# Ten gate and value pairs per layer from seven half-block products

## The chip, the cores and the metric

One core of one Trainium2 chip runs the kernel; the other cores are idle. The metric is the device time of the whole program in microseconds. The kernel before took 1496.4 us (median of 3 runs, 1495.83 to 1497.2). The engines are named as in the profile: PE (TensorE, matmuls) with PEld (its weight loads), DVE (VectorE), ACT (ScalarE), POOL (GpSimd) and SP (SyncE, which issues the DMAs).

## The reference

A trunk of four residual steps over 512 positions of width 1024, in two layers. Layer 0 mixes with a gated short convolution and differential attention, layer 1 with stick-breaking attention; each layer then attends into 256 memory tokens and applies a gated feed-forward block. Only the feed-forward block is touched here:

```python
D_FF = 2816                       # w_up: 1024 x 5632, w_down: 2816 x 1024

def rmsnorm(x, g):
    y = x * lax.rsqrt(jnp.mean(x * x, axis=-1, keepdims=True) + EPS)
    return y * g

def causal_dwconv(x, w):          # width 3, over positions
    ...

def conv_ffn(h, w_up, w_conv, w_down):
    u = causal_dwconv(h @ w_up, w_conv)
    gate, val = jnp.split(u, 2, axis=-1)
    return (jax.nn.silu(gate) * val) @ w_down

x = x + conv_ffn(rmsnorm(x, norm_ffn[l]), ffn_w_up[l], ffn_conv[l], ffn_w_down[l])
```

All is fp32.

## The kernel before

Activations lie transposed: 8 tiles `x` of 128 channels by 512 positions. Every fp32 operand is carried as two float32r parts, `hi` (a rounded copy, made by ACT) and `lo` (operand minus `hi`, made by DVE; `split`). A product of two operands is then three matmuls into one PSUM accumulator: `hi`x`hi`, `hi`x`lo`, `lo`x`hi`.

Weights come from HBM in slots of 128 x 1024, in the order in which they are used (`weight_groups`), through three `raw` buffers (`loads`); `prep` splits each slot into a `hi` and a `lo` tile (five buffers each). `lin` walks a group: for each chunk of 128 output columns it takes an accumulator `acc` (three PSUM buffers), and `lin_stream` issues 24 matmuls (8 blocks of 128 input channels, three each) of 128 x 128 weights against 512 positions. PSUM has three more pools: `sc` (two buffers), `tr` (two) and `pv` (one), which the attention stages use and the feed-forward stage leaves alone.

In the feed-forward stage of a layer (`ffn`) the up-projection has 22 pairs, chunk j (gate) and chunk 22 + j (value). The kernel before loads two pairs as one group `U` (a = 0 to 10). The normalising factor of a position, 1/rms, is a row (`rrow`) that is known late; the operand split into `hs` tiles is therefore x times the gain alone, and each finished chunk is multiplied by `rrow` on DVE (`c<-acc,rrow`). Three convolution steps follow (one on ACT, two on DVE), Silu on ACT for a gate, the product of the two on DVE, and a split for the down-projection. The down-projection runs in three blocks of 8, 8 and 6 of the 22 inner tiles, `D`; each adds its result to `x` (`x<-x,acc`). The first down block follows up group 4 (pairs 0 to 9), the others come near the end.

The order of work on each engine is fixed when the program is built: `Issue.run` plays streams of operations (loads, prep, one stream per accumulator, follow-up work) against costs and latencies, and appends to each engine's list the operation that can start first, with a priority where several can. On the chip every engine then takes its list strictly in that order and waits on semaphores. So a change in one place may reorder what comes later.

Names in the profile are those of tiles, with the buffer numbers left out. Lines that matter: L441 `tensor_tensor`, L449 `scalar_tensor_tensor`, L426 a copy or cast on ACT, L429 an ACT function, L479 the matmul, L483 a transpose. In the changed kernel these lines stand three lower (L444, L452, L429, L432, L482, L486).

Of the kernel before, what the change touches and what calls it, by code (L numbers as in the profile page):

```python
# [32 lines left out]
SORDER = ("q0", "v0", "q1", "q2", "v1", "q3")  # L33


def weight_groups():

    def c(*starts):
# [20 lines left out]
    def common(l):  # L59
        for a in range(2):  # L60
            g.append((f"Q{a}_{l}", "x_w_q", l, ks, c(*range(4 * a, 4 * a + 4))))
        for a in range(2):
            g.append((f"XO{a}_{l}", "x_w_out", l, ks[4 * a:4 * a + 4], c(*range(8))))

        def up(a):
            g.append((f"U{a}_{l}", "ffn_w_up", l, ks, c(2 * a, 22 + 2 * a, 2 * a + 1, 22 + 2 * a + 1)))

        def dn(a, b):
            kk = list(range(8 * a, min(8 * a + 8, 22)))
            g.append((f"D{a}{b}_{l}", "ffn_w_down", l, kk, c(*range(4 * b, 4 * b + 4))))  # L70

        for a in range(5):
            up(a)
        dn(0, 0)
        dn(0, 1)
        for a in range(5, 9):
            up(a)
        dn(1, 0)
        up(9)
        dn(1, 1)  # L80
        up(10)
        dn(2, 0)
        dn(2, 1)

    kv(0)
    common(0)
# [14 lines left out]


GROUPS = weight_groups()
GN = {g[0]: i for i, g in enumerate(GROUPS)}
NSLOT = [len(g[3]) * len(g[4]) * P // SLOT for g in GROUPS]
FIRST = [sum(NSLOT[:i]) for i in range(len(GROUPS) + 1)]

# [36 lines left out]
POW_WAIT = 0.0  # L144

PREP_FIRST, SUM_FIRST, SUM = 0.45, 3.2, 1.5
PE_RATE, PE_FIX = 2400.0, 0.0133


# [228 lines left out]
def trunk(ctx: ExitStack, tc: tile.TileContext, xT: bass.AP, memT: bass.AP, wts: bass.AP, par: bass.AP, outT: bass.AP):  # L378
# [251 lines left out]
    def loads():  # L630
        for gi in range(len(GROUPS)):
            for d in extra.get(gi, ()):
                yield from d()
            for s in range(NSLOT[gi]):
# [10 lines left out]
                    yield dma(raw.v(), src, SLOT)  # L645
                raws[gi, s] = raw

    def prep(groups):
        for gi in groups:
            for s in range(NSLOT[gi]):  # L650
                hi, lo = yield [AL(pHI, F32R, (P, SLOT), parts=2), AL(pLO, F32R, (P, SLOT), parts=2)]
                if gi == 0:
                    for j in range(2):
                        js = slice(j * 512, j * 512 + 512)
                        yield Until(lambda: (gi, s, j) in raws)
                        raw = raws[gi, s, j]
                        yield act(hi[:, js].p(j), raw[:, js].p(j))
                        yield tt(lo[:, js].p(j), raw[:, js].p(j), hi[:, js].p(j).f32(), ALU.subtract)
                        prepped[gi, s, j] = (hi, lo)
                else:  # L660
                    yield Until(lambda: (gi, s) in raws)
                    raw = raws[gi, s]
                    yield act(hi, raw)
                    yield tt(lo, raw, hi.v().f32(), ALU.subtract)
                    prepped[gi, s, 0] = prepped[gi, s, 1] = (hi, lo)
                free(raw)

    def lin_stream(gi, m, kind, A, ps, done, n):
# [29 lines left out]
        if sub is not None:  # L698
            spawn(sub, 1.0)
        fin[gi] = fin.get(gi, 0) + 1  # L700


    used_k = {}
# [588 lines left out]
    def ffn(l, xin, xout, last):  # L1292
        N = norm_x(xin, f"norm_ffn{l}", True)
        acts, own, gate_t = {}, {}, {}

        def up_done(a):
            def done(m, ps):
                j = 2 * a + m // 2
                gate = m % 2 == 0
                u = yield AL(pC)  # L1300
                yield Until(lambda: "rrow" in N)
                yield tt(u, ps, N["rrow"], ALU.mult)
                free(ps)
                t = yield AL(pG)
                yield from conv3(u, f"ffn_conv{l}", j if gate else 22 + j, 44, t)
                free(u)
# [18 lines left out]
                    acts[j] = o  # L1325
            return done

        def up(a):
            yield from lin(f"U{a}_{l}", "f", N["A"], up_done(a))

        names = [xin, ("f0", l), ("f1", l), xout]

        def dn(a, b):
            base = add_x(names[a], names[a + 1], 4 * b)

            def done(m, ps):
                k = 4 * b + m
                if last and a == 2 and k == KD - 1:

                    yield Until(lambda: (names[a], k) in F)  # L1340
                    x = F[names[a], k]
                    for js in (slice(0, S // 2), slice(S // 2, S)):
                        yield tt(x[:, js], x[:, js], ps[:, js], ALU.add)
                        yield dma(outT[k][:, js], x[:, js], S // 2)
                    free(ps)
                    return
                yield from base(m, ps)
# [3 lines left out]
            if b == 1:  # L1351
                def fr():
                    yield lin_done(f"D{a}0_{l}", f"D{a}1_{l}")
# [4 lines left out]
        for a in range(5):  # L1358
            yield from up(a)
        yield from dn(0, 0)  # L1360
        yield from dn(0, 1)
        for a in range(5, 9):
            yield from up(a)
        yield from dn(1, 0)
        yield from up(9)
        yield from dn(1, 1)
        yield from up(10)

        def nfree():
            yield lin_done(f"U10_{l}")  # L1370
            hs_free(N)
            yield Until(lambda: 21 in acts)
            free(N["r"], N["rrow"])
        spawn(nfree(), 0.1)
        yield from dn(2, 0)
        yield from dn(2, 1)


    so, sown, sqk, sv, sv_own = {}, {}, {}, {}, {}
# [272 lines left out]
```

## Time and profile before

| | |
|---|---|
| median of 3 runs | 1496.4 us |
| the profiled execution | 1496.61 us |
| its span, first to last instruction | 1494.8 us |
| PE busy | 1488.9 us, 6968 matmuls |
| DVE busy | 1022.3 us, 1625 instructions |
| ACT busy | 725.2 us, 1193 instructions |
| granted clock of PE | 1.00 |

The profile is of one execution. A line of a timeline has the start and length in us, the engine, the source line, the operation, output<-inputs, the shape and a count. A line of the list of groups has the count, then the busy time and the mean length of one in ns. Matmuls are pipelined, so their recorded lengths overlap; what one costs in a row of them is the distance of their starts.

### The profile page before, as it was taken

The page shows a single profiled execution, that of the slowest core. Times are in us where ns is not written, and L with a number is a line of the kernel's source. Part 1 is how long each engine was busy: PE and PEld are TensorE (multiplying, and loading weights), DVE is VectorE, ACT ScalarE, POOL GpSimd, SP SyncE. Part 2 cuts the span into 40 slices and gives each one's busy share as a digit, 9 for nine tenths or more (in the row PEclk, how much of TensorE's full clock was granted, in tenths as well). Part 3 has the DMA queues.
Part 4 walks back from the last instruction along what each step waited for, and adds up shares of the span by engine and source line. Part 5 has one row for each costly group of instructions (what it writes and reads, how often), then busy time and mean ns, then how long its engine had stood idle before and what let it go on. Part 6 is the DMA issues. An engine that isn't in the chain of part 4 may idle for free.

```text
span 1494.8 us, 18401 instructions
## 1 busy us (share of the span) xinstructions
PE 1488.9 (100%) x6968; PEld 1240.3 (83%) x6968; DVE 1022.3 (68%) x1625; ACT 725.2 (49%) x1193; POOL 66.1 (4%) x139
## 2 busy tenths in 40 slices
PE   9999999999999999999999999999999999999998
PEld 8888888888888888888888888888888888888887
DVE  7689767565776367555678989857657775567543
ACT  6576456443544144334477877755435443334321
POOL 3210000000000000000100000000000000000000
PEclk9999999999999999999999999999999999999999
DMA  7122436211332333233221221552212333233322
GB/s 234 57 85 71 149 119 190 92 57 57 113 107 78 98 113 90 79 113 112 86 69 59 65 92 57 145 165 85 81 61 70 100 113 113 72 98 113 95 75 85
DMA packets 42711, 146.20 MB, mean 98 GB/s; under 512 B 4864, under 2 KB 5376, under 8 KB 42624
## 3 DMA queue, kind: packets, MB, share of 16 engines
q1 hardware_dynamic: 42624, 145.04, 31.3%
q8 instruction: 55, 0.90, 0.3%
q14 instruction: 32, 0.26, 0.1%
HBM read 142.92 MB, written 2.10 MB: 97 GB/s over the span
## 4 chain that ended last, share of the span: by engine, by line
PE 94%; DVE 3%; ACT 1%; DMA 1%; issue 1%; SPq 0%; DVEq 0%
PE acc L479 85%; PE sc L479 4%; PE pv L479 3%; PE tr L483 3%; DMA raw<-wts 1%; DVE lo L441 0%; DVE g L1408 0%; ACT h L426 0%; DVE g L441 0%; DVE h L441 0%; DVE pt L441 0%; DVE c L441 0%; ACT hi L426 0%; DVE kl L449 0%; SPq L488 0%
## 5 line engine op out<-in xcount | busy, mean ns | idle before, releaser
L479 PE MATMUL acc<-hs,hi 128*128 128x512 f32 x2208 | 690.7, 391 | 0.0
L479 PEld LDWEIGHTS acc<-hs,hi 128*128 128x128 f32 x2208 | 413.4, 188 | 83.2
L479 PE MATMUL acc<-hs,lo 128*128 128x512 f32 x1104 | 430.5, 391 | 0.0
L426 ACT CAST hi<-raw 128x1024 fp32r<-128x1024 f32 (+1 forms) x264 | 273.2, 1039 | 226.2 <-PE acc L479 159.6
L441 DVE TENSOR_TENSOR lo<-raw,hi 128x1024 fp32r<-128x1024 f32 (+1 forms) x264 | 316.9, 1204 | 67.4 <-ACT hi L426 64.5
L479 PEld LDWEIGHTS acc<-hs,lo 128*128 128x128 f32 x1104 | 207.4, 188 | 41.1
L479 PE MATMUL acc<-h,hi 128*128 128x512 f32 x704 | 216.0, 389 | 0.0
L479 PE MATMUL acc<-hi,hs 128*128 128x512 f32 x544 | 176.6, 395 | 0.0
L441 DVE TENSOR_TENSOR x<-x,acc 128x512 f32<-128x512 f32 (+1 forms) x105 | 71.3, 680 | 145.0 <-PE acc L479 145.0
L479 PEld LDWEIGHTS acc<-h,hi 128*128 128x128 f32 x704 | 132.1, 188 | 27.4
L449 DVE SCALAR_TENSOR_TENSOR g<-c,pp,g 128x510 f32<-128x510 f32 (+1 forms) x176 | 131.1, 749 | 29.3 <-ACT g L429 27.1
L479 PE MATMUL acc<-h,lo 128*128 128x512 f32 x352 | 136.1, 389 | 0.0
L441 DVE TENSOR_TENSOR c<-acc,rrow 128x512 f32<-128x512 f32 x92 | 63.4, 691 | 96.6 <-PE acc L479 89.4
L429 ACT ACTIVATE g<-c,pp 128x512 f32<-128x512 f32 x88 | 63.5, 723 | 131.5 <-DVE c L441 131.5
L479 PEld LDWEIGHTS acc<-hi,hs 128*128 128x128 f32 x544 | 101.5, 188 | 20.0 <-DVE hs L449 0.3
L479 PE MATMUL acc<-lo,hs 128*128 128x512 f32 x272 | 106.5, 392 | 0.0
L479 PE MATMUL acc<-y,hi 128*128 128x512 f32 x256 | 81.0, 393 | 0.0
L479 PEld LDWEIGHTS acc<-h,lo 128*128 128x128 f32 x352 | 66.1, 188 | 13.7
L441 DVE TENSOR_TENSOR g<-g,g 128x512 f32<-128x512 f32 (+2 forms) x112 | 63.0, 571 | 3.5 <-ACT g L429 1.4
L429 ACT ACTIVATE g<-sc,rq 128x128 f32<-128x128 f32 (+7 forms) x128 | 62.2, 542 | 3.6 <-PE sc L479 3.3
L479 PEld LDWEIGHTS acc<-lo,hs 128*128 128x128 f32 x272 | 51.3, 189 | 9.8
L426 ACT CAST pt<-tr 128x128 fp32r<-128x128 f32 (+2 forms) x96 | 43.1, 457 | 30.9 <-PE tr L483 30.4
(181 smaller groups left out, 1502.5 us busy)
## 6 DMA issues: line engine op xcount, KB each, us to landing
raw<-wts SPq DMA_DIRECT2D x256, 512.0 KB, 4.1
x<-xT SPq DMA_DIRECT2D x16, 256.0 KB, 5.3
raw<-wts SPq DMA_DIRECT2D x8, 256.0 KB, 5.4
raw<-memT SPq DMA_DIRECT2D x4, 512.0 KB, 3.9
outT<-x SPq DMA_DIRECT2D x7, 256.0 KB, 2.0
outT<-x SPq DMA_DIRECT2D x2, 128.0 KB, 1.7
pp<-par SPq DMA_DIRECT2D x1, 175.5 KB, 4.7
sq<-par SPq DMA_DIRECT2D x1, 128.0 KB, 5.0
```

The lines of the kernel that those rows point to most:

```text
L426: return nc.scalar.copy(out=out.ap, in_=in_.ap)
L429: return nc.scalar.activation(out=out.ap, in_=in_.ap, func=func, scale=_raw(scale), **kw)
L441: lambda: _ve(eng).tensor_tensor(out=out.ap, in0=in0.ap, in1=in1.ap, op=op))
L449: lambda: nc.vector.scalar_tensor_tensor(out=out.ap, in0=in0.ap, scalar=_raw(scalar), in1=in1.ap, op0=op0, op1=op1))
L479: lambda: nc.tensor.matmul(out.ap, lhsT.ap, rhs.ap, start=start, stop=stop))
L483: return Op("PE", 0.109, [in_, ident_v], [out], lambda: nc.tensor.transpose(out.ap, in_.ap, ident_v.ap))
```

## The change

For ten of the 22 pairs of each layer (`SEVEN`: 8, 10, 12, 14 and 16 to 21) the two chunks are no longer formed by 48 matmuls of 512 positions. The pair is seen as a 2 x 2 block product. The positions are halved (256 each), the 8 blocks of input channels are put into two classes (even and odd), and the two chunks are the two output halves. Four such blocks of the weights times four of the activations take eight half products, and the scheme of Winograd and Strassen takes seven, with sums and differences of blocks ahead of them and additions behind. A half product is 4 blocks x 3 parts = 12 matmuls of 256 positions.

- *Weights* (`prep_halved`): both raw slots of the pair are waited for. Slot 0 is split as it is ("a"), and the last quarter alone ("d", into the two `sq` tiles); four additions or subtractions of 512 columns on DVE then turn the raw tiles into sums, which are split too ("b", "c"). Three splits of 1024 and one of 512, in place of two of 1024.
- *Activations* (`fold`): since the sums mix positions, the operand must carry `rrow`. After the last of the first eight pairs the `hs` tiles are made again, with `rrow` in them, and for each of four pairs of blocks the two halved sums are made and split. They go to tiles that the attention stages use (`kl`, `pt`, `so`, `rrow`).
- *Products* (`lin_halved`): the seven use the accumulators acc, sc, pv, tr, sc, tr, sc in this order. One copy on ACT and seven additions of 256 columns on DVE put the two chunks together in `c` tiles.
- The other pairs behind the fold (9, 11, 13, 15) lose their multiplication by `rrow`; their convolution reads the accumulator itself.
- *Order* (`FFN_ORDER`): groups of one pair in place of two; the first down block follows pair 7 instead of pair 9, and the first and second down blocks are cut into four parts of two chunks; the second stands between pairs 17 to 21.

```diff
+UP_SCALED = 8
+FFN_ORDER = ([("u", j) for j in range(8)] + [("d", 0, b) for b in range(4)] + [("u", j) for j in range(8, 17)]
+             + [("d", 1, 0), ("u", 17), ("d", 1, 1), ("u", 18), ("d", 1, 2), ("u", 19), ("u", 20), ("d", 1, 3), ("u", 21),
+                ("d", 2, 0), ("d", 2, 1)])
+SEVEN = {l: (8, 10, 12, 14, 16, 17, 18, 19, 20, 21) for l in range(2)}
...
+    def prep_halved(gi):
+        lo_, hi_ = slice(0, 512), slice(512, 1024)
+        yield Until(lambda: (gi, 1) in raws)
+        r0, r1 = raws[gi, 0], raws[gi, 1]
+        pair = [AL(pHI, F32R, (P, SLOT), parts=2), AL(pLO, F32R, (P, SLOT), parts=2)]
+        ha, la = yield pair
+        yield act(ha, r0)
+        yield tt(la, r0, ha.v().f32(), ALU.subtract)
+        prepped[gi, "a"] = (ha, la)
+        a11, a12, a21, a22 = r0[:, lo_].p(0), r0[:, hi_].p(1), r1[:, lo_].p(0), r1[:, hi_].p(1)
+        hd, ld = yield [AL(pSQ, F32R), AL(pSQ, F32R)]
+        yield act(hd, a22)
+        yield tt(ld, a22, hd.v().f32(), ALU.subtract)
+        prepped[gi, "d"] = (hd, ld)
+        yield tt(a11, a11, a21, ALU.subtract)
+        yield tt(a21, a21, a22, ALU.add)
+        yield tt(a22, a22, a11, ALU.subtract)
+        yield tt(a12, a12, a22, ALU.subtract)
+        for n, r in (("b", r1), ("c", r0)):
+            h, lo = yield pair
+            yield act(h, r)
+            yield tt(lo, r, h.v().f32(), ALU.subtract)
+            prepped[gi, n] = (h, lo)
+            free(r)
...
+    def lin_halved(gi, N, acc, done):
...
+        def product(ps, slot, off, rhs, last=True):
+            for q in range(4):
+                yield Until(lambda: (gi, slot) in prepped and N.get("folded", 0) > q)
...
+                yield mm(ps, hi[:, cs].p(j), bh, q == 0, False)
+                yield mm(ps, hi[:, cs].p(j), bl, False, False)
+                yield mm(ps, lo[:, cs].p(j), bh, False, q == 3)
...
+        yield from product(acc[:, :256], "a", 0, part(0, t1), last=False)
+        u1, u2 = yield [AL(pC, parts=2), AL(pC, parts=2)]
+        c11, c12, c21, c22 = u1[:, t1].p(0), u1[:, t2].p(1), u2[:, t1].p(0), u2[:, t2].p(1)
+        then(act(c11, acc[:, :256]), lambda: free(acc), flag("p1"))
+        p2 = yield AL(aSC)
+        yield from product(p2[:, :256], "a", 512, part(1, t1))
+        p4 = yield AL(aPV)
+        yield from product(p4[:, :256], "d", 0, sums(1, t1))
+        p6 = yield AL(aTR)
+        yield from product(p6[:, :256], "b", 512, sums(1, t2), last=False)
+        then(Until(lambda: "p1" in st), add(c12, c11, p6), lambda: free(p6), flag("p6"),
+             add(c11, c11, p2), lambda: free(p2))
+        p5 = yield AL(aSC)
+        yield from product(p5[:, :256], "b", 0, sums(0, t1))
+        p7 = yield AL(aTR)
+        yield from product(p7[:, :256], "c", 0, sums(0, t2), last=False)
+        then(Until(lambda: "p6" in st), add(c21, c12, p7), lambda: free(p7), flag("p7"),
+             add(c12, c12, p5), flag("p5"), add(c22, c21, p5), lambda: free(p5),
+             add(c21, c21, p4), lambda: free(p4), lambda: done(1, u2))
+        p3 = yield AL(aSC)
+        yield from product(p3[:, :256], "c", 512, part(1, t2))
+        then(Until(lambda: "p5" in st), add(c12, c12, p3), lambda: free(p3), lambda: done(0, u1))
...
+        def fold():
+            yield lin_done(*(f"U{j}_{l}" for j in range(UP_SCALED)))
...
+            for q in range(4):
+                b1, b2 = yield [AL(pC, parts=2), AL(pC, parts=2)]
+                for k, b in ((2 * q, b1), (2 * q + 1, b2)):
+                    yield stt(b, F[xin, k], pc(f"norm_ffn{l}", k), N["rrow"], ALU.mult, ALU.mult)
+                    N["read"] = k + 1
+                for k, b in ((2 * q, b1), (2 * q + 1, b2)):
+                    hi, lo = N["A"][k]
+                    yield from split(hi, lo, b)
+                x, y, z, w = b1[:, t1].p(0), b1[:, t2].p(1), b2[:, t1].p(0), b2[:, t2].p(1)
+                yield tt(x, y, x, ALU.subtract)
+                yield tt(y, w, y, ALU.subtract)
+                yield tt(w, w, x, ALU.subtract)
+                yield tt(z, z, w, ALU.subtract)
+                for b, (hi, lo) in zip((b1, b2), N["T"][q]):
+                    yield from split(hi, lo, b)
+                free(b1, b2)
+                N["folded"] = q + 1
```

What the change moves on the engines is seen at three places. In the rows, a tile's name carries its own number, so equal numbers are one tile.

PE, up-projection of layer 0, before: the last matmuls of one chunk and the first of the next (`hs` is the activation, `hi` and `lo` the weights).

```order
L479 MATMUL acc_4668<-hs_3653,hi_4721 128x512
L479 MATMUL acc_4668<-hs_3654,hi_4721 128x512
L479 MATMUL acc_4668<-hs_3653,lo_4722 128x512
L479 MATMUL acc_4694<-hs_3559,hi_4605 128x512
L479 MATMUL acc_4694<-hs_3560,hi_4605 128x512
L479 MATMUL acc_4694<-hs_3559,lo_4606 128x512
```

And now, in pair 8: the end of the second product and the start of the third (weights "d" in `sq`, activation sums in `kl`).

```order
L482 MATMUL sc_4672<-hs_3653,hi_4492 128x256
L482 MATMUL sc_4672<-hs_3654,hi_4492 128x256
L482 MATMUL sc_4672<-hs_3653,lo_4493 128x256
L482 MATMUL pv_4689<-kl_4311,sq_4518 128x256 x2
L482 MATMUL pv_4689<-kl_4311,sq_4519 128x256
```

Where an accumulator was filled by 24 matmuls of 512 columns, a half-wide one is filled by 12 of 256, and the next product goes to another pool.

DVE, first down block of layer 0, before: splits of weights (`lo`) and additions to the residual (`x`).

```order
L441 TENSOR_TENSOR x_1819<-x_1819,acc_4388 128x512
L441 TENSOR_TENSOR y_4503<-g_4471,y_4502 128x512
L441 TENSOR_TENSOR x_1821<-x_1821,acc_4423 128x512
L441 TENSOR_TENSOR x_1823<-x_1823,acc_4472 128x512
L441 TENSOR_TENSOR lo_4572<-raw_4461,hi_4571 128x1024
```

And now at that place: the fold for two blocks stands between them (`c` the scaled block, `hs` its new split, `kl` the split of the sums).

```order
L444 TENSOR_TENSOR c_4318<-c_4318 128x256
L444 TENSOR_TENSOR c_4318<-c_4319,c_4318 128x256
L444 TENSOR_TENSOR h_4365<-g_4329,h_4365 128x512
L444 TENSOR_TENSOR c_4319<-c_4319,c_4318 128x256
L444 TENSOR_TENSOR c_4319<-c_4319 128x256
L444 TENSOR_TENSOR lo_4378<-raw_4247,hi_4377 128x1024
L444 TENSOR_TENSOR x_1819<-x_1819,acc_4239 128x512
L444 TENSOR_TENSOR kl_4310<-c_4318,kl_4310 128x512
L444 TENSOR_TENSOR x_1821<-x_1821,acc_4276 128x512
L444 TENSOR_TENSOR kl_4311<-c_4319,kl_4311 128x512
```

The fold's rows share the list with the splits and the additions to x of the down block.

DVE, late in the up-projection of layer 0, before: splits, scalings by `rrow`, convolution steps (`g`).

```order
L441 TENSOR_TENSOR lo_5021<-raw_4896,hi_5020 128x1024
L441 TENSOR_TENSOR c_5040<-acc_4934,rrow_3756 128x512
L441 TENSOR_TENSOR lo_5036<-raw_4925,hi_5035 128x1024
L449 SCALAR_TENSOR_TENSOR g_5047<-c_5040,pp,g_5047 128x511
L449 SCALAR_TENSOR_TENSOR g_5047<-c_5040,pp,g_5047 128x510
L441 TENSOR_TENSOR g_5047<-g_5047,g_4998 128x512
```

And now: the additions of pair 19 (`c` from `tr`, `sc`, `pv`) between the weight sums (`raw`) and splits of pair 20.

```order
L444 TENSOR_TENSOR c_6129<-c_6129,tr_6159 128x256
L444 TENSOR_TENSOR raw_6051<-raw_6051 128x512
L444 TENSOR_TENSOR c_6129<-c_6129,sc_6131 128x256
L444 TENSOR_TENSOR raw_6051<-raw_6051,raw_5937 128x512
L444 TENSOR_TENSOR raw_5937<-raw_5937,raw_6051 128x512
L444 TENSOR_TENSOR c_6130<-c_6129,tr_6191 128x256
L444 TENSOR_TENSOR c_6129<-c_6129,sc_6176 128x256
L444 TENSOR_TENSOR c_6130<-c_6130,sc_6176 128x256
L444 TENSOR_TENSOR lo_6212<-raw_6051,hi_6211 128x1024
L444 TENSOR_TENSOR c_6130<-c_6130,pv_6146 128x256
```

The scalings are gone; the additions that release `tr`, `sc` and `pv` now stand in one list with another pair's weight sums and splits.

More of the change, by code (lines that the diff above doesn't have):

```diff
@@ L1356, in dn @@
                 spawn(fr(), 0.1)
[L1358 to L1367, printed above, removed]
         def nfree():
-            yield lin_done(f"U10_{l}")
+            yield lin_done(*(f"U{j}_{l}" for j in range(22)))
             hs_free(N)
+            free(*N["own"])
             yield Until(lambda: 21 in acts)
@@ L1374, in ffn @@
         spawn(nfree(), 0.1)
-        yield from dn(2, 0)
-        yield from dn(2, 1)
+        spawn(fold(), FOLD)
+        for step in FFN_ORDER:
+            yield from (up if step[0] == "u" else dn)(*step[1:])
     so, sown, sqk, sv, sv_own = {}, {}, {}, {}, {}
```

98 lines of the change are left out of this document (70 added, 28 removed).

## The prediction

> **What bounds the kernel now.** I read the page first: the engines' busy shares and the chain that ended last.
>
> ```profile
> span 1494.8 us, 18401 instructions
> PE 1488.9 (100%) x6968; PEld 1240.3 (83%) x6968; DVE 1022.3 (68%) x1625; ACT 725.2 (49%) x1193; POOL 66.1 (4%) x139
> ...
> PE 94%; DVE 3%; ACT 1%; DMA 1%; issue 1%; SPq 0%; DVEq 0%
> ```
>
> TensorE has work in all of the span, and the chain runs through it. A full busy bar alone doesn't prove a bound, because matmul records overlap; so next I read the chain in order of time, in the feed-forward stage of layer 0.
>
> ```profile
> 389.37 351.18 PE acc L479 x1549
> ```
>
> One unbroken piece: 1549 matmuls of 512 columns in 351.18 us, that is 0.2267 us each, with nothing else on the chain. Here the time is the number of matmuls times their pitch, and a shorter list of matmuls shortens the span one for one, as long as the other engines keep up. What they have left shows in the stretches of the two feed-forward stages (columns: stretch and its length; busy time of PE, PEld, DVE, ACT, POOL with counts; clock; DMA share; GB/s). The middle row is another stage, used below.
>
> ```profile
> 385.00:760.00 375.00, 375.00 (x1670) 310.67 (x1669) 237.11 (x302) 150.30 (x198) 5.55 (x14) 1.00 0.31 95
> 810.00:870.00 60.00, 59.67 (x316) 49.81 (x315) 59.19 (x102) 52.88 (x108) 5.22 (x28) 1.00 0.22 66
> 1120.00:1491.00 371.00, 371.00 (x1641) 306.81 (x1639) 227.38 (x286) 133.50 (x166) 1.01 (x1) 1.00 0.30 93
> ```
>
> The granted clock is 1.00. VectorE is busy 237 of 375 us and 227 of 371 us, so about 140 us per layer lie open on it; ScalarE and the DMA queues have more.
>
> **TensorE's part of the sum.** A gate and value pair took 2 chunks x 8 blocks x 3 matmuls = 48 of 512 columns: 48 x 0.2267 = 10.88 us. It becomes 7 products x 4 blocks x 3 = 84 of 256 columns. The columns fall by 7/8, but matmuls rise by 36, so all hangs on the pitch of a 256-wide matmul with a new weight load each. The cross-attention scores have that shape (timeline of PE: start, length, count), with the group of their weight loads behind:
>
> ```profile
> 274.00 2.04 PE L479 MATMUL sc<-y,h 128*128 128x256 f32 x15
> 275.88 0.40 PE L479 MATMUL acc<-hs,hi 128*128 128x512 f32 x1
> ...
> 1064.15 1.95 PE L479 MATMUL sc<-y,h 128*128 128x256 f32 x15
> 1065.94 0.40 PE L479 MATMUL acc<-hs,hi 128*128 128x512 f32 x1
> ...
> L479 PEld LDWEIGHTS sc<-y,h 128*128 128x128 f32 x192 | 26.0, 190 | 1.4
> ```
>
> From the first start to the next group's start: 1.79 us / 15 = 0.119 in the later run, 1.88 / 15 = 0.125 in the earlier one. I take 0.120, near the run without a hole. A pair then costs 84 x 0.120 = 10.08 us, 0.80 less, and 20 pairs (ten in each of two layers) give **-16.0 us**. The ends: at 0.119, 10.00 and -17.6; at 0.125, 10.50 and -7.6. Exactly half of a 512-wide one (0.1134) would give 9.53 and -27; no run shows it, so I keep it as a far bound. All other matmuls stay: the order has 720 more in sum, which is 20 x 36.
>
> The Trainium skill, "TensorE: Matmul & The Clock Gate", section "Back-to-back issue gap", gives 131 ns per matmul at 512 columns and 81 ns at 128 in a stream of loads and matmuls; by a straight line between them, an estimate of 98 ns at 256, a pair would go from 6.3 to 8.2 us and the change would lose some 39 us. The chain's 226.7 ns at 512 columns contradicts that, so it gets no weight beyond the last rival below.
>
> **VectorE's part.** How fast it takes instructions is read from neighbouring starts, not from recorded lengths:
>
> ```profile
> 482.58 0.74 DVE L449 SCALAR_TENSOR_TENSOR g<-c,pp,g 128x510 f32<-128x510 f32 x1
> 483.24 1.22 DVE L441 TENSOR_TENSOR lo<-raw,hi 128x1024 fp32r<-128x1024 f32 x1
> ...
> 486.19 1.53 DVE L449 SCALAR_TENSOR_TENSOR g<-c,pp,g 128x511 f32<-128x511 f32 x2
> ...
> 921.38 1.22 DVE L441 TENSOR_TENSOR lo<-raw,hi 128x1024 fp32r<-128x1024 f32 x1
> 922.51 1.00 DVE L1408 TENSOR_TENSOR_SCAN g<-g,g 128x128 f32<-128x128 f32 x2
> ...
> 928.97 0.41 DVE L441 TENSOR_TENSOR pt<-tr,pt 128x256 fp32r<-128x256 f32 x1
> 929.31 0.67 DVE L441 TENSOR_TENSOR g<-g,g 128x511 f32<-128x511 f32 x1
> 929.91 0.99 DVE L1408 TENSOR_TENSOR_SCAN g<-g,g 128x128 f32<-128x128 f32 x2
> ```
>
> Start to start: 1.13 us for 1024 columns, 0.60 for 512, 0.34 for 256, 0.66 for the three-operand form; each next one starts some 0.08 us before the recorded end. Where an instruction needs the one just before it (the two at 486.19: 1.53 - 0.75), it is 0.78 instead of 0.66, so 0.12 more.
>
> A pair cost VectorE before: 2 splits of 1024 (2.26), 2 scalings (1.20), 4 convolution steps (2.64), product and split (1.20): 7.3 us. A halved pair: 3 splits of 1024 (3.39), one of 512 and 4 weight sums (3.00), 7 additions of 256 (2.38), convolution 2.64, product and split 1.20: 12.6 us, and about 7 dependent steps more, 13.4. So it needs more of VectorE than the 10.08 us that TensorE gives it. A plain pair behind the fold loses its scaling: 6.1. The fold of the activations is 4 x (2 x 0.66 + 4 x 0.60 + 4 x 0.34) = 20.3 us per layer. By stages, TensorE against VectorE:
>
> - up 0 to 7: 87.0 against 58.4.
> - the first down block, where the fold lies: 192 x 0.2267 = 43.5 against 20.3 + 8 x 1.13 + 8 x 0.60 = 34.1.
> - up 8 to 16 (5 halved, 4 plain): 93.9 against 87.4, or 91.4 with the dependent steps.
> - up 17 to 21 with the second down block: 93.9 against 76.9, or 81.
> - the last down block: 32.6 against 11.6.
>
> Every stage fits, the third just. That VectorE can run so full is what the 810 to 870 row shows: 59.19 of 60 us busy, while TensorE kept 59.67. Nor can the fold be late by much harm: it starts when the eighth pair's last matmul is done, and the 43.5 us of the down block cover its 34.1; without that cover its 20.3 us per layer would stand on the path.
>
> Within a pair the tight place is the two-buffer score pool, which products 2, 5 and 3 share. Product 3 may only start when product 2 has been added up, which stands behind the addition of product 6. From product 6's end TensorE has products 5 and 7 to do, 24 x 0.120 = 2.88 us; VectorE needs two additions, 0.68 us, so 2.2 us are over, against the 0.60 of the one instruction that the order puts between the two additions in pair 19. Only pairs 19 and 20 stand back to back, and there the single buffer of product 4 is read late, behind a 1024 split (1.13). I book **+1.5 us** over both layers for such late additions, about what the 0.33 us of that full stretch would be for the 188 us of the third and fourth stages (0.33 x 188 / 60 = 1.0 per layer), a little less because VectorE is less full here.
>
> ScalarE and the loads cost nothing on the path:
>
> ```profile
> L426 ACT CAST hi<-raw 128x1024 fp32r<-128x1024 f32 (+1 forms) x264 | 273.2, 1039 | 226.2 <-PE acc L479 159.6
> ...
> raw<-wts SPq DMA_DIRECT2D x256, 512.0 KB, 4.1
> ```
>
> A halved pair adds about 1.75 columns-thousand of copies to ScalarE, 1.8 us by this row, on an engine that is busy 40% here. The number of loads is the same. A pair now holds two of three raw buffers until its last splits, so the next pair's second slot is asked for late; the 4.1 us it takes are covered by the 6 us of additions, convolution and products (2.38 + 2.64 + 1.20) that VectorE does for the pair after its splits. If that cover were gone, VectorE would start the next pair's splits up to 4.1 us late, and TensorE after it.
>
> **Sum.** -16.0 + 1.5 = -14.5. The profiled execution took 1496.6 us with a span of 1494.8; 1496.6 - 14.5 = 1482.1, so a span near 1480.3. The median shown is 0.2 under the profiled execution: **1482.0 us**.
>
> **Rivals.** *VectorE becomes the bound.* If it took recorded lengths (1.22, 0.67, 0.41, 0.75), a halved pair is 14.2 us and a plain one 6.8: the third stage needs 98.2 against 93.9, and TensorE stands 4.3 us per layer. -16.0 + 8.6 = -7.4: 1489.0. For it speaks that the third stage is within 3 us of full; against it that starts lie closer than lengths. The Trainium skill, "VectorE: DVE Perf Modes", section "The DRAIN you can't avoid", says that the next operation does not start until the pipe is empty, and adds that one which is not held starts earlier. The first would make this rival true; the start at 922.51, 0.09 before the end of the instruction at 921.38, follows the second.
>
> *A round trip through the accumulators, on the slower side.* Product 3 waits for the addition of product 2, and the next product 4 for its single buffer. If at both places an addition gets stuck behind one more 1024 split than there is room for, TensorE stands 1.13 us twice per pair: 20 x 2.26 = 45 us, -16 + 45 = +29: 1525.4. It decides from 0.80 us of standing per pair. For it: VectorE runs its list strictly in order, with splits between the additions. Against it: 2.2 us of room, and a plain pair or a down block between nearly all halved ones.
>
> *The pitch has holes.* Seven products start in seven buffers; if each brings one hole like that in the 1.88 us run (0.09), a pair is 10.7, and -3.4 + 1.5 gives 1494.5. For it: one of the two runs has a hole. Against: 1549 matmuls with none, though they change buffers every 24.
>
> *Weight loads come to the surface.* A load is recorded at 190 ns, more than the 120 of the matmul that has to cover it; at 0.19 a pair is 16.0, +5.1, and the time 1598. Both runs of 15 speak against it.
>
> **How the numbers follow.** The forecast, TensorE bound at 0.119 to 0.125 with up to 4 us of waits, has 0.74; VectorE as the bound 0.10; holes 0.08; the round trip 0.06; loads 0.02. The range: low end at a pitch of 0.1175, a little under the faster run (9.87, -20.2), with 1.5 of waits, 1477.7; high end at 0.125 (-7.6) with 1.6 of waits, 1490.4, which takes in VectorE as the bound. About 0.2% (3 us) can be told from no change: faster 0.74 + 0.10 + half of the holes = 0.88; the other half 0.04 as the same; slower 0.08.
>
> **What would show it.** Right: 1680 matmuls of 256 columns with starts 0.120 apart; TensorE's pieces of the chain still unbroken from the first up pair to the end; VectorE's busy time up by some 160 us by recorded lengths, without TensorE waiting for it. Wrong: pieces of VectorE in the chain between up 8 and up 21; a 256-wide pitch over 0.125; gaps before the products in the score pool or product 4's buffer.

## The result and the profile after

| | before | after |
|---|---|---|
| median, us (lowest to highest, 4 runs each) | 1496.47 (1495.83 to 1497.2) | 1480.56 (1480.36 to 1480.94) |
| ratio, 95% interval | | 0.9894 (0.9877 to 0.9911) |
| span of the profiled execution, us | 1494.8 | 1478.8 |
| busy DVE / ACT, us | 1022.3 / 725.2 | 1152.2 / 776.3 |

The change makes the kernel 15.9 us faster; the forecast was 1482.0 with a range of 1477.7 to 1490.4. The spans differ by 16.0 us, which is TensorE's term of the sum to the tenth. The head of the page after, and its chain's shares by engine:

```profile
span 1478.8 us, 20262 instructions
PE 1471.9 (100%) x7688; PEld 1260.9 (85%) x7688; DVE 1152.2 (78%) x1909; ACT 776.3 (52%) x1285; POOL 66.1 (4%) x139
...
PE 96%; DVE 2%; ACT 1%; issue 0%; DMA 0%; SPq 0%; DVEq 0%; ACTq 0%
```

TensorE has 720 more matmuls in 17.0 us less of busy time, and its share of the chain rose. The chain in order of time, in layer 0 (start, length, what), from the plain up pairs over the first down block to the first halved pair:

```profile
388.83 118.22 PE acc L482 x527
507.04 1.44 PE sc L482 x12
508.48 1.44 PE pv L482 x12
509.92 1.44 PE tr L482 x12
511.36 1.44 PE sc L482 x12
512.80 1.44 PE tr L482 x12
514.24 1.44 PE sc L482 x12
515.68 12.34 PE acc L482 x60
```

The first row ends with pair 8's first product, which stands in an `acc` buffer. Then come its six other products, named by their PSUM pools, each 12 matmuls in 1.44 us, so 0.120 us apart, and each starting where the one before it ends. The last row is a plain pair (48 x 0.2267 = 10.88) and the next first product (1.44). So a halved pair takes 10.08 us and nothing is lost between seven buffers. In both layers the chain is TensorE alone from here to the end of the last down block. The stretches by stage (length; busy time of PE, PEld, DVE, ACT, POOL; clock; DMA share; GB/s): up 8 to 16, up 17 to 21 with the second down block, and the last down block:

```profile
505.60:599.50 93.90, 93.90 (x614) 86.33 (x613) 83.53 (x127) 46.66 (x64) 0.00 (x0) 1.00 0.33 102
599.50:693.40 93.90, 93.90 (x613) 86.33 (x613) 76.88 (x118) 41.05 (x53) 0.00 (x0) 1.00 0.32 98
693.40:726.00 32.60, 32.60 (x146) 27.01 (x145) 25.45 (x37) 18.55 (x27) 0.00 (x0) 1.00 0.33 106
```

TensorE works through all three without a hole, and the first two are 93.9 us long, as the sum had them. VectorE is open for 10 us and 17 us of them.

### The profile page after: what moved, and what is told of

It is laid out like the page before. It is cut to its first block, busy times and chain, and to the rows that moved or that the text cites. A ratio compares the mean times of both kernels' runs of the same rounds, so it can differ in the third digit from the quotient of the medians.

```text
span 1478.8 us, 20262 instructions
## 1 busy us (share of the span) xinstructions
PE 1471.9 (100%) x7688; PEld 1260.9 (85%) x7688; DVE 1152.2 (78%) x1909; ACT 776.3 (52%) x1285; POOL 66.1 (4%) x139
## 4 chain that ended last, share of the span: by engine, by line
PE 96%; DVE 2%; ACT 1%; issue 0%; DMA 0%; SPq 0%; DVEq 0%; ACTq 0%
PE acc L482 74%; PE sc L482 10%; PE pv L482 5%; PE tr L482 4%; PE tr L486 3%; ACT h L429 0%; DVE lo L444 0%; ACT g L432 0%; DMA x<-xT 0%; DVE h L444 0%; DVE c L444 0%; DVE g L444 0%; DVE g L1534 0%; DVE kl L452 0%; ACT pt L429 0%
## 5 line engine op out<-in xcount | busy, mean ns | idle before, releaser
L482 PE MATMUL acc<-hs,hi 128*128 128x512 f32 (+1 forms) x1728 | 524.4, 382 | 0.0
L429 ACT CAST hi<-raw 128x1024 fp32r<-128x1024 f32 (+1 forms) x284 | 294.0, 1039 | 246.6 <-PE acc L482 105.0
L444 DVE TENSOR_TENSOR lo<-raw,hi 128x1024 fp32r<-128x1024 f32 (+1 forms) x284 | 341.3, 1206 | 79.8 <-ACT hi L429 77.1
L482 PEld LDWEIGHTS acc<-hs,hi 128*128 128x128 f32 x1728 | 318.9, 188 | 59.2
L482 PE MATMUL acc<-hs,lo 128*128 128x512 f32 (+1 forms) x864 | 329.6, 382 | 0.0
L482 PEld LDWEIGHTS acc<-hs,lo 128*128 128x128 f32 x864 | 162.6, 188 | 28.6
L482 PEld LDWEIGHTS acc<-hi,hs 128*128 128x128 f32 x544 | 101.3, 188 | 20.8 <-ACT hs L432 1.2
L452 DVE SCALAR_TENSOR_TENSOR g<-c,pp,g 128x511 f32<-128x511 f32 (+1 forms) x144 | 102.1, 746 | 3.7 <-ACT g L432 2.8
L432 ACT ACTIVATE g<-c,pp 128x512 f32<-128x512 f32 x72 | 49.5, 718 | 19.7 <-DVE c L444 19.7
L482 PE MATMUL sc<-hs,hi 128*128 128x256 f32 x320 | 59.3, 283 | 0.0
```

The source lines that it names most:

```text
L429: return nc.scalar.copy(out=out.ap, in_=in_.ap)
L432: return nc.scalar.activation(out=out.ap, in_=in_.ap, func=func, scale=_raw(scale), **kw)
L444: lambda: _ve(eng).tensor_tensor(out=out.ap, in0=in0.ap, in1=in1.ap, op=op))
L452: lambda: nc.vector.scalar_tensor_tensor(out=out.ap, in0=in0.ap, scalar=_raw(scalar), in1=in1.ap, op0=op0, op1=op1))
L482: lambda: nc.tensor.matmul(out.ap, lhsT.ap, rhs.ap, start=start, stop=stop))
```

## The experiments

Each time is the median of 4 runs (10 with no halved pair and with the tax of three, 2 with the tax of eight). The kernel before took 1495.85 to 1496.24 us beside them. No kernel here changes what is computed. Where pairs are taken out of the table, the sums of the activations are still formed, read or not, and the "tax" repeats one subtraction into the same tile.

**Where the gain comes from: three kernels that do part of the change.** The first empties the table, which leaves the new order of loads, the activations scaled ahead and the fold, but no halved product.

```diff
-SEVEN = {l: (8, 10, 12, 14, 16, 17, 18, 19, 20, 21) for l in range(2)}
+SEVEN = {l: () for l in range(2)}
```

> The changed kernel with no halved pair: the new order of the feed-forward groups, the fold of the activations and the plain pairs behind it stay, but all 22 pairs are formed by 48 matmuls of 512 columns (the sums of activations are still made, and used by nobody). My theory, that the whole gain is the 16.0 us fewer of matmul pitch in the halved pairs: TensorE's list is as long as before, and VectorE has room for the fold, so 1496.5 us, within 1.5. Rival, that the new order or the lost scalings carry a part of the gain: 1481 to 1493. Rival, that the fold is not hidden and the halved pairs gain more than the pitch says: above 1499.

Measured 1495.99, ratio 1.0000 (0.9990 to 1.0009). Its chain in layer 0 is one piece again:

```profile
388.67 351.16 PE acc L482 x1549
```

All that stands round the halved products is worth nothing, and the fold's 20.3 us of VectorE work lie under the first down block as argued. The second keeps only the five pairs that alternate with plain ones.

```diff
-SEVEN = {l: (8, 10, 12, 14, 16, 17, 18, 19, 20, 21) for l in range(2)}
+SEVEN = {l: (8, 10, 12, 14, 16) for l in range(2)}
```

> The changed kernel with five halved pairs per layer (8, 10, 12, 14, 16) in place of ten. If each halved pair is worth its 0.80 us of matmul pitch and nothing stands: 10 x 0.80 = 8.0 off the time before, 1488.5. If the third stage, where these five lie, had VectorE as its bound: less gain, 1490 to 1494.

Measured 1488.36, ratio 0.9949 (0.9934 to 0.9963): 7.9 us under the kernel before, for 10 x 0.80 = 8.0. None, five and ten pairs gain 0.3, 7.9 and 15.9 us, so the gain goes with the number of pairs. The third halves the matmuls of the ten pairs without saving a product: each 512-wide matmul becomes two 256-wide ones, 96 for a pair.

```diff
-SEVEN = {l: (8, 10, 12, 14, 16, 17, 18, 19, 20, 21) for l in range(2)}
+SEVEN = {l: () for l in range(2)}
+HALF = (8, 10, 12, 14, 16, 17, 18, 19, 20, 21)
...
+        if gi in halfwide:
+            for t in (slice(0, 256), slice(256, 512)):
+                for ki in range(nk):
...
+                    ah, al = ah[:, t], al[:, t]
+                    yield mm(ps[:, t], wh, ah, ki == 0, False)
+                    yield mm(ps[:, t], wh, al, False, False)
+                    yield mm(ps[:, t], wl, ah, False, ki == nk - 1)
```

> As the kernel without halved pairs, but the same ten pairs per layer are formed by eight half products: every matmul of 512 columns becomes two of 256 over the same weights, 96 in place of 48 per pair. A matmul's pitch at 256 columns of 0.120 against half of 0.2267 gives 96 x 0.120 - 10.88 = 0.64 more per pair, 20 x 0.64 = 12.8: 1509.3. If halving the columns cost nothing by itself: 1496.5. If the first matmul in each accumulator had a hole of 0.09: some 3 us more.

Measured 1509.62, ratio 1.0090 (1.0075 to 1.0105). Its chain in layer 0:

```profile
388.79 357.74 PE acc L483 x2029
```

2029 is 1549 + 480. The 480 more matmuls cost 357.74 - 351.16 = 6.58 us, 0.66 us for a pair: that is what halving alone costs. Between this kernel and the change lie 29.1 us, 1.45 for a pair, which is the eighth product (12 x 0.120 = 1.44). The 0.80 us is the difference of the two (1.45 - 0.66 = 0.79).

**What VectorE has left: a tax.** Each halved pair repeats its 512-wide subtraction three more times (and eight more in the second kernel, with `range(9)`), 0.60 us each.

```diff
-        yield tt(ld, a22, hd.v().f32(), ALU.subtract)
+        for _ in range(4):
+            yield tt(ld, a22, hd.v().f32(), ALU.subtract)
```

> The changed kernel with three more VectorE instructions of 512 columns per halved pair (the split of the last weight quarter is done four times), 1.8 us of VectorE per pair at a pitch of 0.60, 18 us per layer; TensorE's list is unchanged. If VectorE has room in all stages: 1480.6. By my sums of the third stage without dependent steps (87.4 + 9.0 = 96.4 against 93.9) TensorE stands 2.5 us per layer: 1485.6; with dependent steps (100.4 against 93.9) 6.5 per layer: 1493.6. By recorded lengths (98.2 + 5 x 3 x 0.67 = 108.3) 14.4 per layer: 1509.

> The changed kernel with eight more VectorE instructions of 512 columns per halved pair, 4.8 us of VectorE per pair; TensorE's list is unchanged. Third stage without dependent steps 87.4 + 24 = 111.4 against 93.9, fourth 76.9 + 24 = 100.9 against 93.9: 24.5 per layer late, 1530. With dependent steps (115.4 and 105) 32.6 per layer, 1546. If VectorE had so much room that it never binds: 1480.6.

Measured 1498.21, ratio 1.0015 (1.0006 to 1.0025), with three, and 1588.56, ratio 1.0618 (1.0596 to 1.0639), with eight. None of the numbers on record holds. With three, the change loses 17.6 us, but not spread over the pairs. The same stretches as above, up 8 to 16 and up 17 to 21:

```profile
505.60:599.50 93.90, 93.29 (x606) 85.51 (x605) 85.95 (x134) 45.38 (x62) 0.00 (x0) 1.00 0.30 99
599.50:693.40 93.90, 88.53 (x549) 80.43 (x548) 83.17 (x130) 36.26 (x48) 0.00 (x0) 0.96 0.27 90
```

In the stage that was thought just full, TensorE stands 0.61 us only. It stands 5.37 us in the next, where VectorE had more room, and there in one place: product 6 of pair 20, right behind pair 19 with nothing plain between. The timeline of PE (what it idled before the instruction and the releaser in brackets), and then stretches before, in and after that wait:

```profile
667.61 0.28 PE L482 MATMUL pv<-pt,sq 128*128 128x256 f32 x1
672.67 0.80 PE L482 MATMUL tr<-kl,hi 128*128 128x256 f32 x2 [4.79 <-ACT hi L429]
```

```profile
667.50:672.70 5.20, 0.41 (x5) 0.21 (x3) 5.13 (x9) 2.36 (x4) 0.00 (x0) 0.79 0.00 0
672.70:677.30 4.60, 4.01 (x17) 3.72 (x18) 4.25 (x6) 1.81 (x2) 0.00 (x0) 0.50 0.47 131
677.30:684.00 6.70, 6.70 (x46) 6.21 (x46) 4.31 (x9) 3.14 (x4) 0.00 (x0) 1.00 0.63 216
```

The starts are 5.06 us apart, and VectorE is busy for 5.13 of the 5.20 us: it is the engine that is late. Behind the wait the clock is granted at 0.50 for 4.6 us. From 667.61 to 677.40, where the pitch is the old one again, TensorE starts 18 matmuls, 18 x 0.120 = 2.16 us of work, in 9.79 us. Of the 7.6 us lost it stands 5.4 (4.79, and 0.59 for the split itself behind the first two matmuls); the other 2.3 are the half clock. Stage by stage, 0.61 + 5.37 + 2.3 = 8.3 us in layer 0. The same waits of 4.79 and 0.59 us stand in the other layer, so together some 16.6 of the 17.6.

How near the change itself is to this place, its own timeline and chain show, with the same two instructions and the cast ahead of them under the tax behind:

```profile
656.70 0.62 ACT L429 CAST sq<-raw 128x512 fp32r<-128x512 f32 x1 [2.39 <-PE pv L482]
662.28 1.22 DVE L444 TENSOR_TENSOR lo<-raw,hi 128x1024 fp32r<-128x1024 f32 x1
666.86 1.44 PE tr L482 x12
```

```profile
661.14 0.62 ACT L429 CAST sq<-raw 128x512 fp32r<-128x512 f32 x1 [3.04 <-DMA raw<-wts]
672.79 3.49 DVE L444 TENSOR_TENSOR lo<-raw,hi 128x1024 fp32r<-128x1024 f32 x3
```

In the change the split that product 6 needs ends at 663.5, 3.4 us before product 6 starts: that is all the cover pair 20 has. Under the tax the cast that begins pair 20's second slot comes at 661.14, behind a load that came late (its raw buffer was held by pair 19's splits), where it was 656.70 behind a freed `sq` buffer. The chain under the tax does not pass through that load:

```profile
660.61 1.45 PE tr L482 x12
...
666.37 2.65 DVE g L452 x4
...
672.87 1.15 DVE lo L444
...
674.06 2.50 PE tr L482 x10
```

It goes from the last matmul of pair 19's product 7 (at 662.06) through 11.9 us of VectorE's list: pair 19's additions, the repeated splits, its four convolution steps, pair 20's four weight sums, and then the split. In the change the weight sums stand ahead of that addition and the convolution steps behind the split. The order is made anew when the program is built, so the tax brought another order with it. The split starts 10.5 us later, for 3.6 us of tax in the two pairs: a cliff, not a slope. How much of it is the tax itself and how much the other order was not separated.

With eight, nearly every halved pair waits and the clock falls again and again, which the expectation had left out. Against the change TensorE stands 69 us more, where 49 to 65 were expected, and it is busy 39 us longer, which fits a mean clock of 0.976 over 1587 us.

To see if that place is all, the next kernel keeps the three and takes pair 20 out of the table:

```diff
-SEVEN = {l: (8, 10, 12, 14, 16, 17, 18, 19, 20, 21) for l in range(2)}
+SEVEN = {l: (8, 10, 12, 14, 16, 17, 18, 19, 21) for l in range(2)}
...
-        yield tt(ld, a22, hd.v().f32(), ALU.subtract)
+        for _ in range(4):
+            yield tt(ld, a22, hd.v().f32(), ALU.subtract)
```

> The kernel with three more VectorE instructions per halved pair, with pair 20 formed in the plain way, so that no two halved pairs follow each other. Theory after the first runs: VectorE binds only where a halved pair follows another at once (13.1 us of VectorE against 10.08), not over a stage; then nothing stands here, and the time is that of the change plus 2 x 0.80 for the two pairs given up: 1482.2. Rival, that the stage sums bind: the third stage is as full as with the tax before, 17.6 us over the change less what pair 20 gives back, 1490 to 1498.

Measured 1483.86, ratio 0.9919 (0.9904 to 0.9934). Two pairs less are worth 1.6 us, so 1480.56 + 1.6 = 1482.2 is what it would take if the tax were free: 1.7 us are left of 17.6. That is near the theory and far from the rival with the stage sums. The same two stretches:

```profile
505.60:599.50 93.90, 93.29 (x606) 85.48 (x605) 85.72 (x133) 45.46 (x62) 0.00 (x0) 1.00 0.31 98
599.50:693.40 93.90, 93.90 (x571) 84.45 (x570) 81.80 (x122) 40.67 (x52) 0.00 (x0) 1.00 0.35 113
```

The second is whole again. The 0.61 in the first, which comes in both layers, is the fifth halved pair's product 6 (pair 16), behind a plain pair. Its chain runs from the end of that plain pair's last chunk (589.78) through the chunk's convolution steps and pair 16's weight sums, which alternate in VectorE's list, to the split (594.88). So the theory that nothing stands where a plain pair lies between is not quite right: the order of the list counts there too.

**More pairs.** All fourteen pairs behind the fold, and twelve (13 and 15 added, so that 12 to 16 follow each other):

```diff
+SEVEN = {l: tuple(range(8, 22)) for l in range(2)}
...
+SEVEN = {l: (8, 10, 12, 13, 14, 15, 16, 17, 18, 19, 20, 21) for l in range(2)}
```

> The changed kernel with all 14 pairs behind the fold halved (8 to 21) in both layers. By TensorE's list alone 8 pairs more at 0.80: -6.4, 1474.2. By VectorE: 14 x 13.4 + 8 x 1.13 + 8 x 0.60 = 201.4 us in the third and fourth stage against 14 x 10.08 + 43.5 = 184.6, so up to 16.8 late per layer, less a lead of some 3: about 1502. Without dependent steps 190.2 against 184.6: about 1480 to 1485.

> The changed kernel with twelve halved pairs per layer (13 and 15 too). By TensorE's list alone -3.2: 1477.4. By VectorE with dependent steps 12 x 13.4 + 2 x 6.1 + 13.8 = 186.8 against 186.3 over both stages, but pairs 12 to 17 stand without a plain pair between them (6 x 13.4 + 3.5 = 83.9 against 71.4 up to there): some waits, 1478 to 1490. If VectorE has more room than I count: 1477.4.

Measured 1531.68, ratio 1.0239 (1.0217 to 1.0260), and 1506.18, ratio 1.0072 (1.0055 to 1.0088). Both are far outside of what was expected: two more pairs in a layer, worth -3.2 us, cost 25.6. Three stretches of 13 us with twelve, in the run of pairs that follow each other, and an addition that comes once in each pair:

```profile
562.00:575.00 13.00, 10.19 (x85) 9.98 (x84) 12.55 (x24) 5.30 (x9) 0.00 (x0) 1.00 0.17 54
575.00:588.00 13.00, 12.12 (x86) 11.72 (x85) 10.71 (x19) 5.34 (x8) 0.00 (x0) 0.87 0.26 82
588.00:601.00 13.00, 10.27 (x85) 10.21 (x84) 12.67 (x22) 6.22 (x9) 0.00 (x0) 1.00 0.29 83
```

```profile
582.03 0.42 DVE L444 TENSOR_TENSOR c<-c,tr 128x256 f32<-128x256 f32 x1 [2.23 <-PE tr L482]
595.12 0.42 DVE L444 TENSOR_TENSOR c<-c,tr 128x256 f32<-128x256 f32 x1 [0.29 <-PE tr L482]
```

TensorE does one pair's 84 matmuls in each stretch, but these two additions come 13.09 us apart; in the periods before and behind, where TensorE runs part of the time at half clock, it is 15.75 and 14.40. TensorE stands some 3 us in two of the stretches. The chain in the 13.09 us, and their row:

```profile
586.30 2.64 DVE g L452 x4
...
589.55 1.15 DVE lo L444
...
590.74 1.46 PE tr L482 x10
...
593.64 1.45 PE tr L482 x12
```

```profile
582.03:595.12 13.09, 10.36 (x86) 10.16 (x85) 12.76 (x22) 6.13 (x9) 0.00 (x0) 1.00 0.23 60
```

It is a loop between the two engines. Product 7's last matmul lets an addition go; behind that addition VectorE's list has 8.7 us of work down to the next pair's split; product 6 waits for that split, and from there to the end of the next product 7 TensorE needs 4.4 us. VectorE is busy for 12.76 of the 13.09 us, within the 12.6 to 13.4 that the prediction gave it for a halved pair. In the period before, it waits 2.23 us for product 7 itself, so it isn't simply full. What was missing in the expectations is that back to back this loop and the fallen clock set the pace, whatever room the stage has as a whole.

**One addition later.** The rival with the round trip: the addition that frees product 2's score buffer is put behind product 7's.

```diff
-        then(Until(lambda: "p1" in st), add(c12, c11, p6), lambda: free(p6), flag("p6"),
-             add(c11, c11, p2), lambda: free(p2))
+        then(Until(lambda: "p1" in st), add(c12, c11, p6), lambda: free(p6), flag("p6"))
...
         then(Until(lambda: "p6" in st), add(c21, c12, p7), lambda: free(p7), flag("p7"),
+             add(c11, c11, p2), lambda: free(p2),
```

> The changed kernel with one addition moved: product 2 is added up after product 7's addition in place of right behind product 6's, so product 3, which needs product 2's accumulator, can only start when two additions behind product 7's last matmul are done. The round trip's price: the way from PE to VectorE, 2 x 0.34, and the way back, together some 0.9 to 1.3 us per pair if VectorE is free, 20 x = 18 to 26: 1499 to 1507, and more where a split stands ahead. If other matmuls fill the wait or the accumulator is free earlier than I think: 1480.6.

Measured 1481.69, ratio 0.9904 (0.9889 to 0.9918). A miss: 1.1 us over the change, where some 20 were expected unless other matmuls filled the wait. Its chain in the first halved pair:

```profile
512.92 1.44 PE tr L482 x12
514.36 1.84 PE acc L482 x8
516.20 1.43 PE sc L482 x12
```

Between product 7 (`tr`) and product 3 (`sc`) stand 8 matmuls of the next plain chunk (`acc`, 8 x 0.23). The order is made when the program is built, and where product 3 can't be due yet it takes matmuls that are. So the run doesn't show what a late addition costs; it shows that this kernel has something to put in its place.

**The four weight sums on GpSimd,** which takes 4 x 0.60 = 2.4 us of a halved pair from VectorE; first with the change's ten pairs, then with twelve and fourteen.

```diff
-        yield tt(a11, a11, a21, ALU.subtract)
-        yield tt(a21, a21, a22, ALU.add)
-        yield tt(a22, a22, a11, ALU.subtract)
-        yield tt(a12, a12, a22, ALU.subtract)
+        yield tt(a11, a11, a21, ALU.subtract, eng="POOL")
+        yield tt(a21, a21, a22, ALU.add, eng="POOL")
+        yield tt(a22, a22, a11, ALU.subtract, eng="POOL")
+        yield tt(a12, a12, a22, ALU.subtract, eng="POOL")
```

> The changed kernel with the four weight sums of 512 columns of each halved pair on GpSimd in place of VectorE. TensorE's list is unchanged and nothing stood in it, so no gain is to be had: 1480.6 if GpSimd keeps up. A one-operand step of 512 columns took GpSimd 0.88 us; with two operands I guess 1.2 to 1.8, so 5 to 7 us per pair on the way to product 6. Pairs 19 and 20, which have some 2 us of room there, may stand 1 to 4 us per layer: 1480.6 to 1489. If GpSimd and VectorE slow each other: more.

> Twelve halved pairs per layer with the weight sums on GpSimd. VectorE's part of a halved pair falls from 13.1 to some 10.7 us, near TensorE's 10.08, so halved pairs may follow each other: if VectorE's time was what stood in the kernel with twelve (25.6 us over the change), most of it goes, and by TensorE's list it is 1477.4; 1477 to 1485. If the way over GpSimd is what is late then (5 to 7 us of sums in a row instead of 2.4): 1490 to 1510.

> All 14 pairs behind the fold halved, weight sums on GpSimd. By TensorE's list 1474.2; VectorE 14 x 10.7 + 13.8 = 163.6 against 184.6, but eight pairs in a row at 10.7 against 10.08 are 5 us late per layer: 1474 to 1484. If the way over GpSimd is what is late: 1500 to 1530, as without GpSimd (1531.7).

Measured 1481.86, ratio 0.9906 (0.9892 to 0.9921); 1508.92, ratio 1.0081 (1.0062 to 1.0099); 1527.59, ratio 1.0207 (1.0190 to 1.0224). With ten it is 1.3 us slower than the change, inside the range on record. With more pairs it gives no relief worth the name (1506.18 and 1531.68 without it), and both times lie in the ranges on record for a late way over GpSimd. With twelve, the group of GpSimd's sums, a stretch in the run of halved pairs, and two VectorE instructions of the kinds that took 1.22 and 0.74 us before:

```profile
L444 POOL TENSOR_TENSOR raw<-raw,raw 128x512 f32<-128x512 f32 x72 | 104.4, 1450 | 468.8 <-DVE lo L444 215.4 <-DMA raw<-wts 214.8 <-DVE sq L444 22.4
```

```profile
570.00:582.00 12.00, 11.37 (x94) 11.12 (x94) 12.00 (x18) 6.10 (x10) 3.99 (x3) 1.00 0.30 89
```

```profile
570.52 1.67 DVE L444 TENSOR_TENSOR lo<-raw,hi 128x1024 fp32r<-128x1024 f32 x1
565.24 1.44 DVE L452 SCALAR_TENSOR_TENSOR g<-c,pp,g 128x510 f32<-128x510 f32 x1
```

And one group of convolution steps in the two kernels with twelve pairs, first with the sums on VectorE, then on GpSimd:

```profile
L452 DVE SCALAR_TENSOR_TENSOR g<-c,pp,g 128x511 f32<-128x511 f32 x80 | 57.6, 745 | 2.9 <-ACT g L432 2.9
L452 DVE SCALAR_TENSOR_TENSOR g<-c,pp,g 128x511 f32<-128x511 f32 x80 | 69.9, 899 | 4.7 <-ACT g L432 4.7
```

A sum takes 1.45 us there, so the four in a row 5.8 instead of 2.4 us, and they lie between a slot's landing and the splits that need them. Yet no piece of GpSimd stands on the chain. In the run of halved pairs, from 560.7 to 588.2, the chain goes through VectorE almost without a break, and VectorE is busy for all of the 12 us shown: some of its steps take longer beside GpSimd's sums, and that uses up the room that the sums left. Behind that, loads stand on the chain (four pieces, 20.8 us over both layers), where there are none in this stage with twelve pairs and the sums on VectorE; that the slower sums hold the raw buffers longer would explain it. Which of the two counts for more was not separated.

## Why the prediction was right, step by step

- **TensorE bounds the kernel, and the matmuls' pitch is the price:** right. 84 x 0.120 = 10.08 against 10.88, twenty times: -16.0 forecast, -16.0 between the spans. Half the pairs gave half of it (1488.36), none gave none (1495.99), and halving without the saved product gave the loss that the pitch demands (1509.62).
- **Late additions, +1.5 us:** mis-sized; they cost 0. The chain has no gap in a pair. The number was carried over from a stretch of another stage in which VectorE was 99% busy; here it is 89% and 82% busy in the two stages. This is the whole error of the sum: 1482.0 - 1480.56 = 1.4.
- **The fold is hidden:** right (1495.99 with all of it and no halved pair).
- **VectorE's price of a halved pair, 12.6 to 13.4 us:** right, 12.76 us busy in the period of 13.09 at full clock. The stage sums built on it gave the right answer for this change, but they are the wrong view for where the limit lies. They called the third stage just full, and it took 1.8 us more per pair with 0.61 us lost. The place that gives way most is pair 20 behind pair 19, in the stage that they called easy. The prediction named these two pairs, but looked there at an addition read late; what is late is the split for product 6, behind whatever the list puts ahead of it.
- **Busy time of VectorE up by some 160 us:** the forecast added up recorded lengths, and so added up over all groups of the two traces the rise is 152.7 (1242.6 - 1089.9). The page's busy time, in which overlapping lengths don't count twice, rose by 129.9 (1152.2 - 1022.3).
- **A held raw buffer is covered:** right for the change, where no load stands on the chain of this stage. Under the tax one slot's cast came behind a late load, 4.4 us later (661.14 against 656.70), but VectorE was waiting for product 7 until 662.06 all the same. With the tax of eight, and with the sums on GpSimd, loads do stand on the chain here (with the tax of eight two, of 4.8 and 5.6 us), so the cover can be lost, as the prediction said.
- **Rivals.** *VectorE as the bound:* not in the change. With two more pairs or 1.8 us more per pair TensorE does wait for VectorE's list, but at single places and in the loop with product 7, not because a stage is full. *The round trip:* no wait of 0.80 us per pair, and moving the addition behind another one did not make one, since other matmuls fill in; its price of 45 us stays untested. *Holes in the pitch* and *weight loads at the surface:* false; 12 matmuls in 1.44 us in each of the seven buffers, although a load is recorded at about 190 ns. The Trainium skill, "TensorE: Matmul & The Clock Gate", section "Back-to-back issue gap", gives 131 ns at 512 columns and 81 ns at 128 for such a stream; the traces here show 226.7 ns at 512 and 120 ns at 256, so its figures do not hold for this kernel.

None of the versions tried beats the change. Left open: if eleven halved pairs, or an order that leaves plain work between 19 and 20 as well, would gain; and if the same tax in an order held fixed, or more halved pairs with the split put ahead of the convolution steps, would cost less.

## What to carry to other kernels

Where one engine is busy without a hole and the others are not, an algorithm that trades its work for theirs can be priced from two pitches: here seven products of half width against eight of full width, 84 x 0.120 against 48 x 0.2267, and the half width alone would have lost. What the other engine can bear is read not from the sum over a stage but from the longest run of expensive pieces without a cheap one between them, from the lead that it has before that run, and from what its list puts between the last product of one piece and the first operand of the next. Put a small tax on the engine that is next in line before adding more: it shows the places that give way, and here the largest was not in the fullest stage. Where the order is made by a program, look at the order of the taxed kernel too, since it can be another.

## What the runs showed of the hardware that was not expected

- **A wait can cost more than its length.** After 5.06 us without a matmul start the granted clock was 0.50 for about 4.6 us, so the wait cost 2.3 us more. With the tax of eight this is 39 us on top of 69 us of standing. The Trainium skill, "TensorE: Matmul & The Clock Gate", section "What's actually happening", says that the clock goes to half after an idle window of about 3.4 us, which this wait agrees with. Shorter waits brought it too, but not each time. With twelve pairs, waits of 2.81 and 0.88 us close together did (the 0.87 in the middle stretch). Of the next two, each alone, the one of 2.73 us did not (the clock in its stretch, 588 to 601, is 1.00) and the one of 2.68 us did:

```profile
590.74 0.39 PE L482 MATMUL tr<-kl,lo 128*128 128x256 f32 x1 [2.73 <-DVE lo L444]
603.83 0.58 PE L482 MATMUL tr<-kl,lo 128*128 128x256 f32 x1 [2.68 <-DVE lo L444]
601.00:614.00 13.00, 10.32 (x63) 9.61 (x62) 11.39 (x18) 6.55 (x9) 0.00 (x0) 0.87 0.49 161
```

What decides between the two, the runs don't show.
- **The pitch of 256-wide matmuls is more than half that of 512-wide ones:** 0.120 against 0.2267, so 0.013 us are lost for each cut; the kernel that only halves the matmuls shows the same, 6.58 us for 480 cuts.
- **VectorE slows beside GpSimd:** 1.67 against 1.22 us for a 1024-wide split and 1.44 against 0.74 for a convolution step, in the kernel with twelve pairs and the sums on GpSimd. Over the whole of that kernel the 80 steps of one convolution group take 899 ns in the mean against 745 with the sums on VectorE. Not every instruction beside a sum is longer, and no run was made to find out which.
